# Six places for a delta rule's decay tiles, attention's transposes through a diagonal, and the w_o casts moved into a merge

## The chip, the cores and the metric

The kernel runs on one core of one Trainium2 chip. The metric is device time in microseconds (us) of one execution, as the median of several runs. The core's engines work from their own in-order queues: PE (TensorE, matrix products), DVE (VectorE), ACT (ScalarE), POOL (GpSimd), and SP (SyncE), which here issues nearly all DMAs. An instruction that waits for a semaphore holds everything behind it on its own queue.

## The reference

One layer of a hybrid diffusion backbone: a half-step SwiGLU FFN, two parallel mixers whose results are merged by sigmoid gates, and a second FFN. There are 512 latent tokens, 256 context tokens and 1024 channels. What the change touches is the delta rule, the attention and the merge:

```python
# gated delta rule, by chunks, in two directions, 4 heads
lower = np.tril(np.ones((GDN_CHUNK, GDN_CHUNK), dtype=bool))
decay = jnp.exp(jnp.where(lower, g[..., :, None] - g[..., None, :], -jnp.inf))
m = jnp.where(strict, jnp.einsum('...ik,...jk->...ij', k_beta, k) * decay, 0.0)
uw = lax.linalg.triangular_solve(jnp.eye(GDN_CHUNK) + m, rhs, lower=True, unit_diagonal=True)
...  # scan over the chunks:  o = (q k^T * decay) v_new + (q exp g) S

# neighbourhood attention, 8 heads of 64: 128 local keys in a window and 256 context keys, one softmax
s = jnp.concatenate([s_loc.reshape(bsz, n_heads, width, n_loc), s_ctx], axis=-1).astype(jnp.float32)
p = jax.nn.softmax(s, axis=-1).astype(v.dtype)
return (jnp.einsum('bhwij,bhiwjd->bhwd', p_loc, v_win) + jnp.einsum('bhwn,bhnd->bhwd', p[..., n_loc:], v_ctx))

def branch_merge(o_a, o_b, gate_a, gate_b, w_pa, w_pb, w_o):
    y = jax.nn.sigmoid(gate_a) * (o_a @ w_pa) + jax.nn.sigmoid(gate_b) * (o_b @ w_pb)
    return y @ w_o
```

## The kernel before, in words

The stages follow each other: FFN 1, the input projections, the delta rule's preparation, the delta rule itself (about 743 to 990 us), attention (about 994 to 1093 us), the merge with `w_pa` (1093 to 1120 us), `w_o`, a layer norm, and FFN 2 (to 1529 us). A planner with a cost for each instruction and due times sets the order on every engine once, when the kernel is built; on the chip each engine then keeps that order. Changing one part of the code can therefore move rows of other parts.

Big products are done in three passes: `split` makes of each weight tile `wr` a rounded high part `wh` (a cast on ACT, L135) and a rest `wl` (a subtraction on DVE, L137), and PE multiplies high by high, low by high and high by low (L190, L191, L192). A weight tile takes the way DMA, ACT cast, DVE subtraction, PE.

**Delta rule.** There are three groups (`grams(0)`, `grams(1)`, `grams(2)`) of four grams each, two chunks by two pairs of heads. A gram (`gram`) loads its decays `Dt` from DRAM (`gcd`, L918; 256 KB, each row spread over 128 partitions), subtracts and masks on DVE (four `scalar_tensor_tensor`, L921), exponentiates on ACT (L922), and multiplies PE's products `pq` by it on DVE (`Bt`, L927; for chunks with an output also `At`, L931). `Bt` goes to DRAM (`bd`, L928). After the four grams of a group `base_inverse` reads the blocks back (`Ltr`, `L`, L947), and inverts 32x32 blocks on DVE row by row, in 62 instructions (`bt`, L954, and `Xt`, L955). `Xt` goes through DRAM (`rd`, L959) and comes back as `T` (L976), which DVE transposes (L978), and then PE builds the whole inverse (`pi`, L857). These parts of different groups are interleaved. The tile `Dt` has two buffers for all twelve grams, so gram n+2 loads when gram n has used its own. While this runs, PE does the rest of the input projections as filling work (`fills`, tiles `pm`, written out as `spill` by ACT, L609), until these run out.

**Attention.** 4 pairs of heads `m` by 4 blocks of columns `b` make 16 units. In each, PE makes the scores `sc` (L1240), DVE adds the bias (L1242) and takes the row maximum (L1244), ACT exponentiates into `pr` with the row sums (L1248, twice 128x512), DVE takes the reciprocal `sm` (L1249), POOL multiplies `pr` by it (L1251, twice 128x512), PE transposes `pr` (L1255, eight of 128x128 with `ident`), ACT copies them to `pT` (L1257), and PE multiplies by the values into `po` (L1266). In eight slots between the units PE does a 128x512 product with `w_pb`, and DVE adds it to `yb` (L1302).

**Merge.** Eight products with `w_pa` (a weight of 128x512 each: `wh`, `wl`), a gate on DVE (L1333), an addition to `yb` on POOL (L1334), and the split of `yb` into `yh`, `yl`. The eight weight tiles of `w_o` (128x1024) are also loaded and split here and before (`wso.fill`).

Of the kernel before, what the change touches and what calls it, by code (L numbers as in the profile page):

```python
# [58 lines left out]
def body(ctx, tc, I, out, dbg=None):  # L59
# [72 lines left out]
    def split(src, hi, lo, behind=()):  # L132

        with tc.issue_after(behind[0]) if behind else nullcontext():
            S.copy(hi, src)  # L135
        with tc.issue_after(behind[1]) if behind else nullcontext():
            V.tensor_tensor(lo, src, hi.bitcast(F32), ALU.subtract)  # L137
# [16 lines left out]
    class Stream:  # L154
# [7 lines left out]
        def fill(self, n):  # L162
            while len(self.q) < n and self.i < len(self.srcs):
# [11 lines left out]
                split(raw[:, 0:c], hi[:, 0:c], lo[:, 0:c], self.behind.get(self.i, ()))  # L175
# [737 lines left out]

    def gram(p, s, bd, g):

        mats = mats_of(s)
        Dt = tl(gb_, [P, 4, P], "Dt", 2)
        nc.sync.dma_start(Dt[:], bass.AP(gcd.tensor, gcd.offset + (4 * s + 2 * p) * P, [[0, P], [24 * P, 2], [1, 2 * P]]))  # L918
        for m, (d, c, i) in enumerate(mats):
            msk = cst[:, (C_MF if d == 0 else C_MB):][:, 0:P]  # L920
            V.scalar_tensor_tensor(Dt[:, m], Dt[:, m], gcum[:, d, s, 2 * p + i:2 * p + i + 1], msk, op0=ALU.subtract, op1=ALU.add)  # L921
        S.activation(Dt[:], Dt[:], AF.Exp)  # L922
        Bt, At = tl(gq, [P, 4, P], "Bt", NBT), None
        for n, t in enumerate(products(p, s)):
            if n == 0:
                for m, (d, c, i) in enumerate(mats):
                    V.scalar_tensor_tensor(Bt[:, m], t[m] if s == 1 else t[:, m], beta[:, d, s, 2 * p + i:2 * p + i + 1], Dt[:, m], op0=ALU.mult, op1=ALU.mult)  # L927
# [115 lines left out]
    oaccs = [tl(gq, [P, 4, 2, P], f"oacc{p}") for p in range(2)]  # L1043

    def scan_step(p, s, Tt, At, Sst):
        cf, cb = FWD_CH[s], BWD_CH[s]
        mats = mats_of(s)
        oacc = oaccs[p]
# [32 lines left out]
        if s >= 2:  # L1081
# [10 lines left out]
            if s < 4:  # L1092
                V.tensor_tensor(oacc[:, cf - 2], ot[:, 0:2], o2[:, 0:2], ALU.add)
                V.tensor_tensor(oacc[:, cb - 2], ot[:, 2:4], o2[:, 2:4], ALU.add)
            else:
                V.tensor_tensor(ot[:], ot[:], o2[:], ALU.add)
                G.tensor_tensor(oacc[:, cf - 2], oacc[:, cf - 2], ot[:, 0:2], ALU.add)
                G.tensor_tensor(oacc[:, cb - 2], oacc[:, cb - 2], ot[:, 2:4], ALU.add)
        return Sn

    def gdn_out(p):

        oacc = oaccs[p]
        for t2 in range(2):
            o = oacc[:, 2 * t2:2 * t2 + 2].rearrange("p t i c -> p (t i) c")
# [6 lines left out]
        for i in range(2):  # L1112
            ps = tl(pgq, [P, 4, P], "pc", 2)
            for t in range(4):
                mt(ps[:, t, :], oacc[:, t, i, :], ident)
# [32 lines left out]
    step(base)  # L1148
    scan_of(0, 0)
# [78 lines left out]
    def attend(m, qa, ka, kc, bias, w, between):  # L1228
# [3 lines left out]
        for b in range(4):  # L1232
# [16 lines left out]
            V.reciprocal(sm[:], sm[:])  # L1249
            for i in range(2):  # L1250
                G.tensor_scalar(pr[:, i], pr[:, i], sm[:, i:i + 1], None, op0=ALU.mult)  # L1251
            for i in range(2):
                pt = tl(pg, [P, 4, P], "pt", 2)
                for q in range(4):
                    T.transpose(pt[:, q, :], pr[:, i, q * P:(q + 1) * P], ident)  # L1255
# [74 lines left out]
    for m in range(8):  # L1330
        wso.fill(min(4 + (m + 1) // 2, 7))
        gt, ps = gated("pa", gad, m, oah, oal)
# [358 lines left out]
```

## Time and profile before

| | |
|---|---|
| median of 3 runs | 1527.29 us (1526.62 to 1529.53) |
| the profiled execution | 1530.66 us, its span 1528.8 us, TensorE clock 0.988 |
| busy: PE, weight loads, DVE, ACT, POOL | 1462.6, 1258.7, 1050.0, 605.4, 226.8 us |
| PE / DVE / ACT / POOL busy from 994 to 1094 us (attention) | 92.41, 63.87, 62.49, 63.75 of 100 us |
| PE / DVE / ACT / POOL busy from 1094 to 1120 us (merge) | 23.23, 21.39, 11.67, 10.27 of 26 us |
| POOL's `pr` by `sm`, L1251 | 32 of 1680 ns in the mean, 53.4 us |

A row of the timeline gives the start, the duration, engine, line, operation, output and inputs, the number of instructions joined, and in brackets the idle time of the engine before it and what ended it. A row of the waits gives the engine with its line, what it waited for, the sum in us, the number of waits, and the longest. DMA times run from issue to landing. The share of PE's busy time is a mean over stages with different limits.

### The profile page before, as it was taken

How to read it: one execution, taken by the hardware profiler on the slowest of the kernel's cores; microseconds unless marked ns; L12 is line 12 of the kernel's file. 1: busy time of each engine (PE TensorE's matmuls, PEld its weight loads, DVE VectorE, ACT ScalarE, POOL GpSimd, SP SyncE). 2: the span in 40 equal slices, each digit the busy share in tenths (PEclk: the TensorE clock that was granted, in tenths of full speed). 3: DMA queues.
4: the chain of work that ended last, by engine and by line, in shares of the span. 5: the costliest groups of instructions: out<-in, count | busy, mean ns of one | idle time of the engine just before them, and what ended most of it. 6: DMA issues, size and time to landing. Idle time of an engine off the chain costs nothing.

```text
span 1528.8 us, 23646 instructions
## 1 busy us (share of the span) xinstructions
PE 1462.6 (96%) x9221; PEld 1258.7 (82%) x9221; DVE 1050.0 (69%) x1792; ACT 605.4 (40%) x1005; POOL 226.8 (15%) x224
## 2 busy tenths in 40 slices
PE   6999999999999999999996899999999999999997
PEld 4779988888888887889875778867678999998886
DVE  8765942597554587768777895576669699886426
ACT  5444221322222255546543444266416444344310
POOL 0000000000000011323301001366421022220001
PEclk9999999999999999999998999999999999999999
DMA  9665742667454334222476634283353143333422
GB/s 370 207 237 180 222 142 97 211 213 260 168 192 146 130 112 137 87 90 79 141 216 180 172 99 122 69 284 117 91 174 138 56 139 102 106 110 139 138 83 83
DMA packets 107586, 230.72 MB, mean 151 GB/s; under 512 B 34177, under 2 KB 47825, under 8 KB 107473
## 3 DMA queue, kind: packets, MB, share of 16 engines
q1 hardware_dynamic: 105312, 221.79, 44.7%
q10 hardware_dynamic: 1586, 5.32, 0.9%
q0 software_dynamic: 576, 2.10, 0.4%
q8 instruction: 72, 1.18, 0.3%
q14 instruction: 40, 0.33, 0.1%
HBM read 206.33 MB, written 22.85 MB: 150 GB/s over the span
## 4 chain that ended last, share of the span: by engine, by line
PE 76%; DVE 10%; DMA 7%; issue 3%; ACT 2%; POOL 2%; SPq 0%; DVEq 0%; ACTq 0%; POOLq 0%
PE ps L209 19%; PE ps L190 8%; PE ps L192 8%; PE ps L191 8%; PE pm L190 5%; PE pm L192 5%; PE pm L191 5%; PE pc L857 2%; PE ps L1478 2%; PE ps L1480 2%; PE ps L1479 2%; DVE wl L137 2%; PE po L1266 1%; DMA T<-rd 1%; PE pt L1255 1%
## 5 line engine op out<-in xcount | busy, mean ns | idle before, releaser
L137 DVE TENSOR_TENSOR wl<-wr,wh 128x1024 fp32r<-128x1024 f32 (+1 forms) x215 | 263.0, 1228 | 195.1 <-ACT wh L135 194.3
L135 ACT CAST wh<-wr 128x1024 fp32r<-128x1024 f32 (+1 forms) x215 | 217.8, 1018 | 333.4 <-PE ps L209 105.0
L192 PE MATMUL ps<-uxh,wl 128*128 128x512 f32 (+1 forms) x496 | 179.6, 363 | 2.2 <-DVE wl L137 2.2
L191 PE MATMUL ps<-uxl,wh 128*128 128x512 f32 (+1 forms) x496 | 179.3, 363 | 0.8 <-DVE uxl L137 0.8
L190 PE MATMUL ps<-uxh,wh 128*128 128x512 f32 (+1 forms) x496 | 179.6, 365 | 0.0
L279 DVE SCALAR_TENSOR_TENSOR adap<-wr,crow 128x1024 f32<-128x1024 f32 x112 | 136.8, 1221 | 38.5 <-DMA wr<-in_w_adaT_dram 37.1
L112 POOL TENSOR_TENSOR rs<-ve,mhalf 128x1 f32<-128x1 f32 (+2 forms) x46 | 50.4, 1099 | 744.6 <-DVE ve L108 735.4
L190 PE MATMUL pm<-uxh,wh 128*128 128x512 f32 x320 | 133.0, 416 | 4.1 <-ACT spill L609 2.1
L192 PE MATMUL pm<-uxh,wl 128*128 128x512 f32 x320 | 128.2, 401 | 0.7 <-DVE wl L137 0.7
L191 PE MATMUL pm<-uxl,wh 128*128 128x512 f32 x320 | 127.8, 399 | 0.0
L192 PEld LDWEIGHTS ps<-uxh,wl 128*128 128x128 f32 x496 | 93.7, 189 | 17.9 <-DVE wl L137 3.3
L191 PEld LDWEIGHTS ps<-uxl,wh 128*128 128x128 f32 x496 | 94.0, 189 | 14.9 <-DVE uxl L137 1.0
L190 PEld LDWEIGHTS ps<-uxh,wh 128*128 128x128 f32 x496 | 93.4, 189 | 14.3 <-issue 0.8
L190 PE MATMUL ps<-uch,wh 128*128 128x256 f32 x352 | 98.6, 280 | 0.0
L192 PE MATMUL ps<-uch,wl 128*128 128x256 f32 x352 | 98.3, 279 | 0.0
L191 PE MATMUL ps<-ucl,wh 128*128 128x256 f32 x352 | 98.2, 279 | 0.0
L209 PE MATMUL ps<-wh,hx 128*128 128x512 f32 x352 | 94.8, 389 | 0.0
L209 PEld LDWEIGHTS ps<-wh,hx 128*128 128x128 f32 x352 | 65.9, 188 | 13.6
L190 PEld LDWEIGHTS pm<-uxh,wh 128*128 128x128 f32 x320 | 61.6, 193 | 16.3 <-ACT spill L609 3.0
L192 PEld LDWEIGHTS pm<-uxh,wl 128*128 128x128 f32 x320 | 61.7, 193 | 14.8 <-DVE wl L137 1.5
L191 PEld LDWEIGHTS pm<-uxl,wh 128*128 128x128 f32 x320 | 61.6, 192 | 10.6
L190 PEld LDWEIGHTS ps<-uch,wh 128*128 128x128 f32 x352 | 66.1, 188 | 0.6
(411 smaller groups left out, 3438.7 us busy)
## 6 DMA issues: line engine op xcount, KB each, us to landing
wr<-in_w_adaT_dram SPq DMA_DIRECT2D x88, 512.0 KB, 4.7
wr<-in_up_dram SPq DMA_DIRECT2D x80, 512.0 KB, 4.2
wr<-in_dn_dram SPq DMA_DIRECT2D x58, 512.0 KB, 3.5
wr<-in_win_dram SPq DMA_DIRECT2D x52, 512.0 KB, 3.9
rb<-in_up_dram SPq DMA_DIRECT2D x18, 512.0 KB, 3.7
wr<-in_w_o_dram SPq DMA_DIRECT2D x8, 512.0 KB, 4.0
ac<-in_up_dram SPq DMA_DIRECT2D x6, 512.0 KB, 5.2
Dt<-gcd SPq DMA_DIRECT2D x12, 256.0 KB, 5.1
```

The source lines that it names most:

```text
L112: G.tensor_tensor(rs[:], ve[:], mhalf[:, 0:n], ALU.pow)
L135: S.copy(hi, src)
L137: V.tensor_tensor(lo, src, hi.bitcast(F32), ALU.subtract)
L190: T.matmul(ps, a, uh[:, k, :], start=(k == 0), stop=False)
L191: T.matmul(ps, a, ul[:, k, :], start=False, stop=False)
L192: T.matmul(ps, b, uh[:, k, :], start=False, stop=(k == nk - 1))
L209: T.matmul(banks[t][d][:, c0:c1], a[:, sl], b[:, d * 512 + c0:d * 512 + c1], start=first and j == 0, stop=last and j == 2)
L279: V.scalar_tensor_tensor(pr[:], raw[:], 1.0, crow, op0=ALU.mult, op1=ALU.mult, accum_out=col[:, c:c + 1])
L857: last[0] = T.matmul(*a, **k).ins
L1478: T.matmul(ps[:], a, uh[:, k], start=k == 0, stop=False)
L1479: T.matmul(ps[:], a, ul[:, k], start=False, stop=False)
L1480: T.matmul(ps[:], b, uh[:, k], start=False, stop=k == 3)
```

## The change

It has three parts. First, the decays of the first two grams stay in the two buffers of `Dt`; the next six (grams 2 to 7 in their order) use four tiles `oacc0` to `oacc3` of the same shape, which take the memory of the two output accumulators (before `[P, 4, 2, P]` twice, now `[P, 4, P]` four times), `oacc0` and `oacc1` twice; the last four grams use `Dt` again. The accumulators are taken only after the second group's grams. For the last group the DVE subtraction is ordered behind the `Bt` product of the gram before it. Second, POOL's multiplication of `pr` goes; DVE makes `dg`, `ident` times 1/sum (two `tensor_scalar` of 128x128 per unit), and the eight transposes become matmuls of `pr` with `dg`. Third, in the merge `wso.fill` stands behind `gated`, and each split of a `w_o` tile is ordered behind the split of the latest `w_pa` tile.

```diff
     def gram(p, s, bd, g):
-        Dt = tl(gb_, [P, 4, P], "Dt", 2)
+        k = (None, None, 0, 1, 2, 3, 0, 1, None, None, None, None)[gram_n[0]]
+        gram_n[0] += 1
+        Dt = tl(gb_, [P, 4, P], "Dt", 2) if k is None else tl(gq, [P, 4, P], f"oacc{k}")
...
-            V.scalar_tensor_tensor(Dt[:, m], ...)
+            with tc.issue_after(bt_last[0]) if s > 3 else nullcontext():
+                V.scalar_tensor_tensor(Dt[:, m], ...)
...
-                    V.scalar_tensor_tensor(Bt[:, m], ...)
+                    bt_last[0] = V.scalar_tensor_tensor(Bt[:, m], ...).ins
...
-    oaccs = [tl(gq, [P, 4, 2, P], f"oacc{p}") for p in range(2)]
+    oaccs = [[], []]
+    def out_of(p, c):
+        return oaccs[p][c // 2][:, 2 * (c % 2):2 * (c % 2) + 2]
...
     base = grams(1)
...
+    for k in range(4):
+        oaccs[k // 2].append(tl(gq, [P, 4, P], f"oacc{k}"))
     scan_of(0, 0)
...
             V.reciprocal(sm[:], sm[:])
+            dg = tl(na_, [P, 2, P], "dg", 2)
             for i in range(2):
-                G.tensor_scalar(pr[:, i], pr[:, i], sm[:, i:i + 1], None, op0=ALU.mult)
+                V.tensor_scalar(dg[:, i], ident, sm[:, i:i + 1], None, op0=ALU.mult)
...
-                    T.transpose(pt[:, q, :], pr[:, i, q * P:(q + 1) * P], ident)
+                    T.matmul(pt[:, q, :], pr[:, i, q * P:(q + 1) * P], dg[:, i], start=True, stop=True)
...
     for m in range(8):
+        gt, ps = gated("pa", gad, m, oah, oal)
+        wso.behind = {j: ws.last for j in range(KT)}
         wso.fill(min(4 + (m + 1) // 2, 7))
-        gt, ps = gated("pa", gad, m, oah, oal)
```

Line numbers differ between the two: L918, L921, L927, L928 and L947 before are L924, L928, L934, L935 and L954 after; L954 and L955 are L961 and L962; L959 is L966; L1249 is L1260; L1268 is L1281; L1302 is L1315; L1333 is L1348.

SP's queue where the first group's grams start; `Dt`, `oacc` are loads of decays, `wr` of weights, `qad`, `kad` and `vcd` are stores, `bd0` the stores of `Bt` (the numbers behind a name are those of buffers and versions). Before:

```order
L811 DMA vcd_886_4988<-vcs_1205_6699 128x256
L613 DMA qad_889_4991<-spill_1215_6763 128x512
L613 DMA kad_890_4992<-spill_1220_6797 128x512
L172 DMA wr_1283_7066<-in_win_dram 128x1024
L928 DMA bd0_1221_6800<-Bt_1224_6809 128x4x128
L918 DMA Dt_1233_6867<-gcd_892_4994 128x2x256
L928 DMA bd0_1221_6800<-Bt_1231_6846 128x4x128
L918 DMA Dt_1240_6904<-gcd_892_4994 128x2x256
```

After:

```order
L812 DMA vcd_886_4988<-vcs_1205_6699 128x256
L924 DMA oacc0_1231_6865<-gcd_892_4994 128x2x256
L924 DMA oacc1_1238_6902<-gcd_892_4994 128x2x256
L614 DMA qad_889_4991<-spill_1213_6761 128x512
L924 DMA oacc2_1277_7043<-gcd_892_4994 128x2x256
L924 DMA oacc3_1293_7133<-gcd_892_4994 128x2x256
L614 DMA kad_890_4992<-spill_1218_6795 128x512
L173 DMA wr_1281_7064<-in_win_dram 128x1024
```

Before, the third and fourth load of decays each stand behind the store of a `Bt`; after, they and the next two stand ahead of every store of a `Bt`.

DVE's queue at the same place. Before:

```order
L137 TENSOR_TENSOR wl_1228_6823<-wr_1226_6820,wh_1227_6822 128x1024
L927 SCALAR_TENSOR_TENSOR Bt_1224_6809<-pq_1225_6810,beta_897_5004,Dt_1223_6802 128x128 x4
L927 SCALAR_TENSOR_TENSOR Bt_1231_6846<-pq_1225_6810,beta_897_5004,Dt_1230_6839 128x128 x4
L921 SCALAR_TENSOR_TENSOR Dt_1233_6867<-Dt_1233_6867,gcum_898_5005,cst_896_5002 128x128 x4
L137 TENSOR_TENSOR wl_1238_6888<-wr_1236_6885,wh_1237_6887 128x1024
L921 SCALAR_TENSOR_TENSOR Dt_1240_6904<-Dt_1240_6904,gcum_898_5005,cst_896_5002 128x128 x4
L927 SCALAR_TENSOR_TENSOR Bt_1234_6874<-pq_1235_6875,beta_897_5004,Dt_1233_6867 128x128 x4
L927 SCALAR_TENSOR_TENSOR Bt_1241_6911<-pq_1235_6875,beta_897_5004,Dt_1240_6904 128x128 x4
L137 TENSOR_TENSOR wl_1285_7069<-wr_1283_7066,wh_1284_7068 128x1024
L921 SCALAR_TENSOR_TENSOR Dt_1279_7045<-Dt_1279_7045,gcum_898_5005,cst_896_5002 128x128 x4
L921 SCALAR_TENSOR_TENSOR Dt_1295_7135<-Dt_1295_7135,gcum_898_5005,cst_896_5002 128x128 x4
L927 SCALAR_TENSOR_TENSOR Bt_1280_7052<-pq_1281_7053,beta_897_5004,Dt_1279_7045 128x128 x4
```

After:

```order
L928 SCALAR_TENSOR_TENSOR oacc0_1231_6865<-oacc0_1231_6865,gcum_898_5005,cst_896_5002 128x128 x4
L928 SCALAR_TENSOR_TENSOR oacc1_1238_6902<-oacc1_1238_6902,gcum_898_5005,cst_896_5002 128x128 x4
L137 TENSOR_TENSOR wl_1226_6821<-wr_1224_6818,wh_1225_6820 128x1024
L934 SCALAR_TENSOR_TENSOR Bt_1222_6807<-pq_1223_6808,beta_897_5004,Dt_1221_6800 128x128 x4
L934 SCALAR_TENSOR_TENSOR Bt_1229_6844<-pq_1223_6808,beta_897_5004,Dt_1228_6837 128x128 x4
L928 SCALAR_TENSOR_TENSOR oacc2_1277_7043<-oacc2_1277_7043,gcum_898_5005,cst_896_5002 128x128 x4
L928 SCALAR_TENSOR_TENSOR oacc3_1293_7133<-oacc3_1293_7133,gcum_898_5005,cst_896_5002 128x128 x4
L934 SCALAR_TENSOR_TENSOR Bt_1232_6872<-pq_1233_6873,beta_897_5004,oacc0_1231_6865 128x128 x4
L137 TENSOR_TENSOR wl_1236_6886<-wr_1234_6883,wh_1235_6885 128x1024
L934 SCALAR_TENSOR_TENSOR Bt_1239_6909<-pq_1233_6873,beta_897_5004,oacc1_1238_6902 128x128 x4
L928 SCALAR_TENSOR_TENSOR oacc0_1310_7232<-oacc0_1310_7232,gcum_898_5005,cst_896_5002 128x128 x4
L137 TENSOR_TENSOR wl_1283_7067<-wr_1281_7064,wh_1282_7066 128x1024
```

The four `scalar_tensor_tensor` of the third and of the fourth gram (`oacc0_1231`, `oacc1_1238`) moved from behind the first two `Bt` to ahead of the weight split `wl_1226` (before `wl_1228`), and those of the next grams stand ahead of the `Bt` of the third.

DVE's queue at the end of attention, from the last slot to the last unit's `oa`. Before:

```order
L1302 SCALAR_TENSOR_TENSOR yb_1696_9364<-gt_1936_10492,pm_1937_10494 128x512
L137 TENSOR_TENSOR wl_1950_10561<-wr_1948_10558,wh_1949_10560 128x512
L1249 RECIPROCAL sm_1940_10512<-sm_1940_10512 128x2
L1268 COPY oa_1945_10540<-po_1882_10256 128x512
L137 TENSOR_TENSOR oal_1693_9361<-oa_1945_10540,oah_1692_9360 128x512
```

After:

```order
L1315 SCALAR_TENSOR_TENSOR yb_1698_9366<-gt_1953_10509,pm_1954_10511 128x512
L137 TENSOR_TENSOR wl_1968_10579<-wr_1966_10576,wh_1967_10578 128x512
L1260 RECIPROCAL sm_1957_10529<-sm_1957_10529 128x2
L1264 TENSOR_SCALAR dg_1958_10533<-ident_2_64,sm_1957_10529 128x128 x2
L1281 COPY oa_1963_10558<-po_1896_10270 128x512
L137 TENSOR_TENSOR oal_1695_9363<-oa_1963_10558,oah_1694_9362 128x512
```

The pair of `dg` stands behind the reciprocal; on POOL the multiplications of `pr` are gone.

DVE's queue at the start of the merge: 128x1024 `wl` are of `w_o`, 128x512 `wl` of `w_pa`, `gt` and `yl` of the merge. Before:

```order
L137 TENSOR_TENSOR wl_1955_10586<-wr_1953_10583,wh_1954_10585 128x1024
L137 TENSOR_TENSOR wl_1968_10642<-wr_1966_10639,wh_1967_10641 128x1024
L1333 SCALAR_TENSOR_TENSOR gt_1951_10564<-gt_1951_10564,pm_1952_10566 128x512
L1333 SCALAR_TENSOR_TENSOR gt_1959_10595<-gt_1959_10595,pm_1960_10597 128x512
L137 TENSOR_TENSOR wl_1958_10592<-wr_1956_10589,wh_1957_10591 128x512
L137 TENSOR_TENSOR wl_1963_10617<-wr_1961_10614,wh_1962_10616 128x512
L137 TENSOR_TENSOR wl_1981_10698<-wr_1979_10695,wh_1980_10697 128x1024
L137 TENSOR_TENSOR yl_1947_10554<-yb_1696_9364,yh_1946_10553 128x512 x2
L1333 SCALAR_TENSOR_TENSOR gt_1964_10620<-gt_1964_10620,pm_1965_10622 128x512
L137 TENSOR_TENSOR wl_1971_10648<-wr_1969_10645,wh_1970_10647 128x512
```

After:

```order
L1348 SCALAR_TENSOR_TENSOR gt_1969_10582<-gt_1969_10582,pm_1970_10584 128x512
L1348 SCALAR_TENSOR_TENSOR gt_1974_10607<-gt_1974_10607,pm_1975_10609 128x512
L137 TENSOR_TENSOR wl_1973_10604<-wr_1971_10601,wh_1972_10603 128x512
L137 TENSOR_TENSOR wl_1978_10625<-wr_1976_10622,wh_1977_10624 128x1024
L137 TENSOR_TENSOR wl_1981_10635<-wr_1979_10632,wh_1980_10634 128x512
L137 TENSOR_TENSOR yl_1965_10572<-yb_1698_9366,yh_1964_10571 128x512 x2
L1348 SCALAR_TENSOR_TENSOR gt_1982_10638<-gt_1982_10638,pm_1983_10640 128x512
L137 TENSOR_TENSOR wl_1986_10660<-wr_1984_10657,wh_1985_10659 128x512
L137 TENSOR_TENSOR wl_1991_10681<-wr_1989_10678,wh_1990_10680 128x1024
L1348 SCALAR_TENSOR_TENSOR gt_1987_10663<-gt_1987_10663,pm_1988_10665 128x512
L137 TENSOR_TENSOR yl_1965_10572<-yb_1698_9366,yh_1964_10571 128x512
```

The two splits of `w_o` that opened the merge are gone from its start, and one stands now behind each second `wl` of `w_pa`.

26 lines of the change are left out of this document (13 added, 13 removed).

## The prediction

> **What bounds the kernel now.** I read the page's engine line and chain first, then PE's waits from 700 to 1200 us, then the timeline of the engines at the longest of these waits.
>
> ```profile
> PE 1462.6 (96%) x9221; PEld 1258.7 (82%) x9221; DVE 1050.0 (69%) x1792; ACT 605.4 (40%) x1005; POOL 226.8 (15%) x224
> PE 76%; DVE 10%; DMA 7%; issue 3%; ACT 2%; POOL 2%; SPq 0%; DVEq 0%; ACTq 0%; POOLq 0%
> ```
>
> PE is busy for 1462.6 of 1528.8 us, and 76% of the chain is PE. No PE work of weight is taken away, so the change can only win part of the 66 us in which PE does nothing, and time in which its clock is low.
>
> ```profile
> PE pi L857 <- DMA T<-rd: 13.0, 2, 12.4
> PE po L1266 <- ACT pT L1257: 4.0, 5, 1.9
> PE pm L192 <- DVE wl L137: 3.4, 4, 1.8
> PE pt L1255 <- POOL pr L1251: 1.3, 2, 0.7
> ```
>
> One wait is 12.4 us, for the first group's inverse to come back from DRAM. The next are in attention (`pT`, `pr`) and in the splits of weights. PE around the long wait:
>
> ```profile
> 786.72 0.50 PE L190 MATMUL pm<-uxh,wh 128*128 128x512 f32 x1 [1.53 <-ACT spill L609]
> 787.78 0.50 PE L192 MATMUL pm<-uxh,wl 128*128 128x512 f32 x1 [0.33 <-DVE wl L137]
> 788.55 0.43 PE pm L191
> 791.11 0.43 PE pm L191
> 795.12 0.23 PE pm L191
> 831.15 0.68 PE L857 MATMUL pi<-T,Bt 32*32 32x32 f32 x32 [12.44 <-DMA T<-rd]
> ```
>
> PE loses 1.53 and 0.33 us and then steps at 0.43 instead of 0.23 us for 9 matmuls (787.78 to 791.54: 3.76 us, where 9 x 0.23 is 2.07), together about 3.5 us. Then its filling work ends near 818.7, and it stands still until 831.15. What it waits for is a chain on DVE and SP:
>
> ```profile
> 749.30 0.33 SPq L613 DMA_DIRECT2D qad<-spill  x1
> 777.18 0.37 SPq L918 DMA_DIRECT2D Dt<-gcd  x1
> 818.49 1.47 SPq L947 DMA_DIRECT2D L<-bd  x2
> 820.06 4.31 SPq L959 DMA_DIRECT2D rd<-Xt  x4
> 826.42 2.02 SPq L976 DMA_DIRECT2D T<-rd  x4
> DMA to landing us min/median/max: 4.0/5.1/5.6
> 753.11 2.16 DVE L927 SCALAR_TENSOR_TENSOR Bt<-pq,beta,Dt 128x128 f32<-128x128 f32 x8
> 763.47 2.15 DVE L927 SCALAR_TENSOR_TENSOR Bt<-pq,beta,Dt 128x128 f32<-128x128 f32 x8
> 776.25 0.16 DVE L954 TENSOR_TENSOR bt<-L,Xt 128x2 f32<-128x2 f32 x1 [3.36 <-POOL L L950]
> 783.28 0.88 DVE L921 SCALAR_TENSOR_TENSOR Dt<-Dt,gcum,cst 128x128 f32<-128x128 f32 x3 [3.00 <-DMA Dt<-gcd]
> 794.74 1.14 DVE L921 SCALAR_TENSOR_TENSOR Dt<-Dt,gcum,cst 128x128 f32<-128x128 f32 x4 [1.11 <-DMA Dt<-gcd]
> 807.59 1.14 DVE L921 SCALAR_TENSOR_TENSOR Dt<-Dt,gcum,cst 128x128 f32<-128x128 f32 x4 [0.77 <-DMA Dt<-gcd]
> 817.40 0.69 DVE L955 TENSOR_REDUCE Xt<-bt 128x16 f32<-128x512 f32 x1
> ```
>
> The base inverse runs on DVE from 776.25 to 818.09. Three times in it DVE stands still for a later gram's decays (3.00, 1.11 and 0.77 us), because their load was issued only when a `Dt` buffer came free, and everything behind on DVE's queue waits along: the inverse itself, and the weight splits of the filling work. Then SP sends `rd` at 820.06, after two loads of `L`, and `T` is back 11 us later.
>
> **The change, part 1: places for the decays.** Three terms.
>
> (a) Inside the first inverse DVE's three waits fall away, 4.88 us. In SP's new order the first two of these loads stand right ahead of the store of `qad` (749.30 now) and the next two right behind it; a load lands 5.1 us after its issue. Two of the three groups of four subtractions move ahead of the inverse, 2 x 1.14 us. By DVE alone `Xt` would end at 818.09 - 4.88 - 2.28 = 810.9.
>
> (b) Before the inverse nothing is won. The third and fourth decay are ready earlier, but the `Bt` of these grams waits for PE's products and for four more groups of subtractions put ahead of it. Counted in the new order from 753 with the rows' durations (8 subtractions 2.28, split 1.22, 8 `Bt` 2.15, 8 subtractions 2.28, 4 `Bt`, split, 4 `Bt`), the fourth `Bt` ends between 765.0 and 766, against 763.47 + 2.15 = 765.6. The inverse begins at 776.25 +- 0.5. Here lies a new wait too: the weight split behind `oacc1`'s subtractions. If these loads land at the median (issue near 749.3, plus 5.1) the split is done near 757.9, about when PE asks for it; at 5.6 or later PE stalls by up to 1.2 us.
>
> (c) What sends `rd` is SP's queue, where the loads of the second group's `L` still stand ahead. They need the last `Bt` of that group, hence PE's pace. PE wins the 3.5 us of 786 to 792, and the loads of `Dt` that SP did in the inverse (0.37 us for the one at 777.18) are gone. So `rd` goes at 820.06 - 4.0 = 816.0, and `Xt`, done by 811 to 814, isn't last any more. I take 4.5 us between this and the 4.88 of the waits. PE still waits some 11 to 12 us at the same place, since its filling work ends earlier by as much. Ends: 0, if the inverse comes no earlier, and 7.2, the waits and the moved subtractions together.
>
> After 831 the first two loads of the third group are early as well, but one more group of subtractions falls into a stage where DVE is the busier engine: +0.5. Part 1: -4.0, from +1 to -7.
>
> **Part 2: attention.**
>
> ```profile
> 994.00:1094.00 100.00, 92.41 (x731) 69.84 (x731) 63.87 (x92) 62.49 (x141) 63.75 (x41) 0.97 0.50 171
> 1086.81 0.17 DVE L1249 RECIPROCAL sm<-sm 128x2 f32<-128x2 f32 x1 [2.26 <-ACT pr L1248]
> 1087.14 3.10 POOL L1251 TENSOR_SCALAR pr<-pr,sm 128x512 f32<-128x512 f32 x2 [2.26 <-DVE sm L1249]
> L1255 PEld LDWEIGHTS pt<-ident,pr x128: 137/140/231, 1002.8 to 1091.3; 128*128 128x128 f32 x128
> L857 PEld LDWEIGHTS pq<-kT x48: 187/192/192, 750.6 to 806.5; 128*128 128x128 f32 x48
> 1092.43 0.54 PE L1266 MATMUL po<-pT,vw 128*64 128x128 f32 x5 [0.73 <-ACT pT L1257]
> 1093.45 0.50 PE L190 MATMUL pm<-oah,wh 128*128 128x512 f32 x1
> 751.03 0.89 PE pq L857 x8
> 548.80 0.87 PE ps L146 x8
> L921 DVE SCALAR_TENSOR_TENSOR Dt<-Dt,gcum,cst x48: 340/346/1397, 743.0 to 860.6; 128x128 f32<-128x128 f32 x48
> ```
>
> In the hundred us PE is busy for 92.41, DVE for 63.87, POOL for 63.75. A unit's POOL step takes 3.10 us between reciprocal and transposes. In the middle of the stage the next unit's scores and the `w_pb` products hide it, but for the 1.3 us of `pr` waits. At the end nothing hides it: the last reciprocal ends at 1086.98, and the last `po` at 1093.45.
>
> `dg` on DVE isn't in the trace. A 128x128 operation with two tensor inputs takes 0.346 us here, a reciprocal of 128x2 0.17; with one tensor input I take 0.2 (nearer to the small one, for its size is fixed cost and a little data), so 0.4 per unit, from 0.34 to 0.7. After the last reciprocal then come 0.4 (`dg`), PE's remaining work of the last two units (four transposes, 16 `po`, eight transposes, 16 `po`: 0.11 us for a transpose by the row of eight, 0.073 for a `po` by the 14 between 1092.43 and 1093.45, so 3.6 from 1086.8 on, partly beside `dg`): the end is near 1090.2, 3.3 earlier. The unit before gets its `pT` earlier too, and with it ACT the last exponentials: 0 to 1 more, I take 0.2. The 1.3 us of waits go. The longest wait for `pT`, 1.9 us in the middle of the stage, I leave as it is, since ACT also works on the next pair's loads there; as a bound, a PE without any of its 7.6 idle us in the stage, with its clock at 1.00 instead of 0.97 for half of it, makes -9. DVE's 32 `dg` (6.4 us, 5 to 11) fall on an engine with 36 idle us, behind a reciprocal that waited for the same sums, so nothing on its queue waits for anything new; cover gone, each unit would pay 0.4.
>
> PE: the page's chain has eight transposes (`ps`, L146) at 0.87 us and eight fp32 matmuls of the same shape (`pq`) at 0.89. So 128 x 0.0025 = +0.3. Part 2: -3.3 - 0.2 - 1.3 + 0.3 = -4.5, from -9 to +1 (no wait won, a dearer `dg` shown at the end of the stage).
>
> One rule speaks against this edit. The Trainium skill (TensorE: Matmul & The Clock Gate, Terms) says that the transpose mode of trn2 is four times faster for FP32; by it a matmul in place of a transpose would cost four times the array time. The two rows above, 0.87 and 0.89, don't show it.
>
> **Part 3: the merge.**
>
> ```profile
> 1101.42 0.50 PE L192 MATMUL pm<-oah,wl 128*128 128x512 f32 x1 [0.95 <-DVE wl L137]
> 1114.18 0.50 PE L192 MATMUL pm<-oah,wl 128*128 128x512 f32 x1 [1.78 <-DVE wl L137]
> 1095.88 2.36 DVE L137 TENSOR_TENSOR wl<-wr,wh 128x1024 fp32r<-128x1024 f32 x2 [0.26 <-ACT wh L135]
> 1099.97 4.23 DVE L137 TENSOR_TENSOR wl<-wr,wh 128x512 fp32r<-128x512 f32 x3
> 1112.38 1.75 DVE L137 TENSOR_TENSOR wl<-wr,wh 128x512 fp32r<-128x512 f32 x1
> ```
>
> PE waits here for DVE's `wl`. Two `w_o` splits (2.36 us of DVE, as much of ACT) lay at 1094.8 to 1098.2, ahead of `w_pa` splits that waited for nothing else; this lets the second weight's split come 2 us earlier and may win the 0.95. But three `w_o` splits now stand between `w_pa` splits, each 1.2 us of DVE (half of the 2.36), and more where POOL adds (a split of 128x512 takes 1.75 at 1112.38); PE has 12 x 0.23 = 2.8 us of work per `w_pa` weight. At two of them I expect 1 us of wait each: -0.95 + 2 = +1.0, from -2 (both waits go) to +3.5 (all three shown in full). FFN 2 has the same instructions in slightly another order: 0 +- 1.
>
> **Sum:** -4.0 - 4.5 + 1.0 = -7.5: the profiled execution's 1530.66 gives 1523.2. That one lies 3.4 above the median of the runs; the median becomes 1527.29 - 7.5 = 1519.8.
>
> **The rivals.** 0.2%, 3 us, is about what a measurement of this kernel can tell from no change.
>
> A. *The wait is only moved in part 1.* `L` of the second group, or a weight split held by the decays, sets `rd` as late as now. For it: 820.06 is 2 us behind `Xt`'s end already. Against it: SP's queue itself followed PE's stall at 786. Part 1 gives +0.5; sum -3.0, 1524.3.
>
> B. *Attention's wait passes to ACT.* ACT is busy for 62.49 of the 100 us, and the largest wait is for `pT`, by name ACT's. Against it: in the tail ACT idles until PE has transposed, and that waits for POOL. Then part 2 gives 0 and the sum is -3.0 again, 1524.3.
>
> C. *`w_o` comes late.* All three moved splits show in full beside POOL at twice their 1.2 us (3 x 2.4), less the 0.95: +6 instead of +1, sum -2.5, 1524.8. Against it: after the merge only the eighth tile is cast late, as before.
>
> D. *Slower: the matmul with `dg` streams at a quarter of the transpose's pace.* 0.11 us becomes 0.44, 128 x 0.33 = 42 us on PE, which is the bound in this stage: 1520 + 42 = 1562. It decides from 0.08 us more per matmul, (7.5 + 3) / 128. For it speaks only that the two rows are of different lines; against it, that `po`, fp32 as well, takes 0.073. This is where the skill's rule named above would lead.
>
> E. *The weight load shows.* A weight load of `pq` takes 192 ns, one of `pt` 140. If 0.05 us each were seen, 6.4 us would go: -1.1, 1526.2.
>
> **How the numbers follow.** The forecast has 0.58, with its own range from 1514 to 1523. A 0.12, B 0.09, A and B together 0.06 (1527.8), C 0.06, D 0.04, E 0.05. Faster by over 0.2% means below 1524.2: 0.57 of the forecast, and half of A and B, and cases better than the forecast are in it already, 0.57 + 0.11 = 0.68; a part of C and E with a better attention adds 0.07: 0.75. Slower: D, and 0.05 of what no row names, mostly a merge at its upper end with A and B: 0.09. The rest, 0.16, is the same. The predicted time is the forecast's, 1519.8. The range goes from 1511 (part 1 at -6 and attention at -9, merge -1) to 1526.2, which takes in A, B, C and E (E at its edge).
>
> **What would show it.** PE's wait for `T` at 826 to 827, still 11 to 12 us long, and no wait of DVE for decays between 776 and 815; `rd` sent near 816. If the wait ends at 831, A holds. POOL almost idle in attention, `dg` at 0.2 us, `pt` eight in 0.9 us (D: 3.5 us), the last `po` 4.5 us nearer to the stage's start. In the merge waits for `wl` at the third and fifth `w_pa` weight. I am wrong at the root if PE's time without work after 994 us doesn't shrink although POOL's step is gone.

## The result and the profile after

The changed kernel takes 1538.87 us (median of 6 runs, 1534.77 to 1540.39), the kernel before 1527.22 in the same comparison: a ratio of 1.0072, 95% interval [1.0058, 1.0087]. It is 11.65 us slower, where 7.5 us less had been forecast; the time lies outside the range. The profiled execution took 1538.53 us, with a span of 1536.7.

The page's engine lines after:

```profile
PE 1476.1 (96%) x9349; PEld 1275.9 (83%) x9349; DVE 1056.1 (69%) x1824; ACT 606.5 (39%) x1005; POOL 177.0 (12%) x192
PE 80%; DVE 10%; DMA 5%; issue 2%; SPq 1%; ACT 1%; POOL 1%; DVEq 0%; POOLq 0%; ACTq 0%
```

POOL gave up 49.8 us, as it should. But PE has 128 instructions more than before (9349 against 9221) and is busy 13.5 us longer, though the code replaced 128 PE instructions by 128 others. PE's waits from 700 to 1200 us:

```profile
PE pi L858 <- DMA T<-rd: 12.8, 3, 10.0
PE pi L858 <- DVE Y L1032: 4.9, 3, 2.4
PE pm L193 <- DVE wl L137: 4.2, 5, 1.8
PE pc L858 <- DVE r L1066: 2.8, 3, 1.4
PE pt L1235 <- ACT pT L1270: 1.6, 1, 1.6
PE po L1279 <- ACT pT L1270: 0.4, 1, 0.4
```

The wait for `pr` is gone and that of `po` for `pT` nearly so (4.0 before); 1.6 us of waiting for `pT` stand at the transposes of the values instead. The longest wait for `T` is 10.0 instead of 12.4, but three of them together are as long as two were.

The same stretches of the program in both kernels, by the view of busy time in windows; a row gives start and end, length, then busy time of PE, weight loads, DVE, ACT and POOL with the number of instructions, TensorE's clock, DMA share and GB/s. Before:

```profile
736.30:831.20 94.90, 79.67 (x400) 66.12 (x399) 65.70 (x180) 36.98 (x56) 9.10 (x25) 0.94 0.69 198
831.20:873.50 42.30, 37.92 (x399) 29.83 (x400) 37.29 (x97) 18.27 (x40) 3.91 (x8) 0.94 0.54 159
873.50:921.90 48.40, 46.64 (x496) 38.72 (x495) 42.54 (x125) 20.27 (x45) 3.32 (x9) 1.00 0.35 99
921.90:994.00 72.10, 69.14 (x646) 59.27 (x644) 40.58 (x91) 26.96 (x59) 19.84 (x27) 0.98 0.33 101
994.00:1093.60 99.60, 92.01 (x730) 69.51 (x730) 63.47 (x92) 62.49 (x141) 63.75 (x41) 0.97 0.50 171
1093.60:1131.90 38.30, 35.53 (x151) 27.78 (x152) 27.94 (x29) 13.87 (x20) 14.32 (x10) 1.00 0.53 165
```

After:

```profile
734.20:824.80 90.60, 77.75 (x398) 65.02 (x396) 64.81 (x176) 36.78 (x54) 9.10 (x25) 0.96 0.71 207
824.80:871.80 47.00, 42.09 (x413) 33.32 (x414) 39.33 (x101) 19.53 (x42) 3.61 (x8) 0.93 0.52 151
871.80:924.30 52.50, 48.83 (x494) 40.35 (x493) 42.88 (x128) 19.84 (x46) 3.43 (x9) 0.93 0.31 85
924.30:997.10 72.80, 67.63 (x632) 57.62 (x631) 39.78 (x88) 26.51 (x59) 19.86 (x27) 0.98 0.33 100
997.10:1106.30 109.20, 105.44 (x858) 85.88 (x857) 70.36 (x123) 62.56 (x141) 10.13 (x9) 0.98 0.47 156
1106.30:1144.70 38.40, 34.41 (x144) 26.58 (x145) 27.85 (x29) 13.95 (x20) 15.35 (x10) 1.00 0.52 168
```

The rows run from the first load of decays to the first inverse on PE, from there to the second `rd`, to the third `rd`, to the first scores (these four are the delta rule), to the last `oa` (attention), and to the first gate after `w_o` (merge and the start of `w_o`). The first stage is 4.3 us shorter, near the 4.5 forecast for it. The next two are 4.7 and 4.1 longer, so that attention starts 5.2 later, counted from the first load. Attention is 9.6 longer, with 128 more PE instructions in it. The merge has not moved. What remains to the end is 4.9 shorter in this pair of profiles; over all profiles below it lies between 392.0 and 396.9 us, for the kernel before too at the upper end, and no cause in the change was found for it. Each of these rows is one execution, and the same kernel's stages differ between executions: the changed kernel's second profile, below, has its scores 4.2 us earlier.

The cause in attention stands in one row of the view by tile. `pt` before and after (minimum, median and maximum in ns):

```profile
L1255 PE MATMUL pt<-ident,pr x128: 270/273/477, 1002.8 to 1091.4; 128*128 128x128 f32 x128
```

```profile
L1268 PE MATMUL pt<-dg,pr x256: 270/275/582, 1005.5 to 1104.2; 128*128 128x128 f32 x128
1095.12 2.05 PE L1268 MATMUL pt<-dg,pr 128*128 128x128 f32 x16
L1264 DVE TENSOR_SCALAR dg<-ident,sm x32: 276/281/1121, 1005.2 to 1099.7; 128x128 f32<-128x128 f32 x32
```

There are 128 such matmuls in the code, and 256 records. The "x16" of the timeline are the eight matmuls of one unit, in 2.05 us, where eight transpositions took 0.87 (the row of `ps` in the prediction): a record is about as long as a transposition was, but each matmul has two.

### The profile page after: what moved, and what is told of

Same layout as the page of the kernel before. It is cut to its first block, busy times and chain, and to the rows that moved or that the text cites. A ratio compares the mean times of both kernels' runs of the same rounds, so it can differ in the third digit from the quotient of the medians.

```text
span 1536.7 us, 23860 instructions
## 1 busy us (share of the span) xinstructions
PE 1476.1 (96%) x9349; PEld 1275.9 (83%) x9349; DVE 1056.1 (69%) x1824; ACT 606.5 (39%) x1005; POOL 177.0 (12%) x192
## 4 chain that ended last, share of the span: by engine, by line
PE 80%; DVE 10%; DMA 5%; issue 2%; SPq 1%; ACT 1%; POOL 1%; DVEq 0%; POOLq 0%; ACTq 0%
PE ps L210 22%; PE ps L191 8%; PE ps L193 8%; PE ps L192 8%; PE pm L191 4%; PE pm L193 4%; PE pm L192 4%; PE ps L1493 3%; PE ps L1494 3%; PE ps L1495 3%; PE pc L858 3%; DVE wl L137 2%; PE pt L1268 2%; PE po L1279 1%; DVE bt L961 1%
## 5 line engine op out<-in xcount | busy, mean ns | idle before, releaser
L280 DVE SCALAR_TENSOR_TENSOR adap<-wr,crow 128x1024 f32<-128x1024 f32 x112 | 136.8, 1221 | 38.4 <-DMA wr<-in_w_adaT_dram 37.0
L210 PE MATMUL ps<-wh,hx 128*128 128x512 f32 x352 | 94.8, 389 | 0.0
```

The source lines that it names most:

```text
L210: T.matmul(banks[t][d][:, c0:c1], a[:, sl], b[:, d * 512 + c0:d * 512 + c1], start=first and j == 0, stop=last and j == 2)
L280: V.scalar_tensor_tensor(pr[:], raw[:], 1.0, crow, op0=ALU.mult, op1=ALU.mult, accum_out=col[:, c:c + 1])
```

## The experiments

All times are medians; the kernel before lay between 1527.1 and 1527.4 us in every comparison. Each kernel also left a profile, so that the same stages could be compared over many kernels. Edits are against the kernel before, if nothing else is said.

### Each part alone, and the matmul by itself

The four kernels are: the decays' part alone (the places together with the rule that orders the last group's subtractions), attention's part alone, the merge's part alone (each is its hunk of the diff), and, for the matmul by itself,

```diff
-                    T.transpose(pt[:, q, :], pr[:, i, q * P:(q + 1) * P], ident)
+                    T.matmul(pt[:, q, :], pr[:, i, q * P:(q + 1) * P], ident, start=True, stop=True)
```

> Only the places for the decays. Theory M (in the changed kernel the matmul with a diagonal costs two passes on PE, and that is the loss): this part alone does not lose, it gives 0 to -5 us; T is back near 821 as in the changed kernel's profile and the scores of attention start no later than before (994). Rival G (the decays' part loses: its lead of 6.4 us at 831 turns into a delay of 3.1 at the start of attention in the changed kernel's profile): +3 us, scores at 997.

Measured: 1533.65, ratio 1.0041 [1.0026, 1.0057]: +6.3 us, more than even rival G said. But the place differs: the first inverse is at 90.8 us after the first decay load (94.9 before), and the scores are at 256.2 (257.7), so in this profile the delta rule lost nothing. Attention, whose code is unchanged, took 103.9 us (99.6), with PE busy 3.8 us longer at a granted clock of 0.92 (0.97). The merge took 43.0 (38.3). About half of that is in ACT's order, in the timeline of this kernel:

```profile
1095.28 2.00 ACT L135 CAST wh<-wr 128x1024 fp32r<-128x1024 f32 x2
1101.03 2.09 ACT L135 CAST wh<-wr 128x1024 fp32r<-128x1024 f32 x3 [3.76 <-DMA wr<-in_w_o_dram]
1102.64 0.50 PE L190 MATMUL pm<-oah,wh 128*128 128x512 f32 x1 [3.00 <-ACT wh L135]
1094.00:1137.00 43.00, 37.95 (x151) 29.85 (x152) 27.98 (x30) 13.77 (x20) 14.31 (x10) 0.92 0.46 145
```

The planner, with other times ahead of it, put a `w_o` cast whose load had not landed before two `w_pa` casts. This is what the third part of the change forbids. In the last row, the same stretch as the last one before, PE is idle for 5.1 us instead of 2.8; but it is also busy for 37.95 instead of 35.53 us, with the same 151 instructions, at a clock of 0.92 instead of 1.00. So the order cost some 2.3 us here and the clock as much.

> Only attention's part: POOL's scaling gone, dg on DVE, transposes as matmuls with dg. Theory M: 128 matmuls x 2 records x 0.11 us = 14 us more PE, less the idle time that POOL's step left (4 to 5 us): +8 to +11 us. Rival G: within 3 us of before.

Measured: 1534.12, 1.0042 [1.0026, 1.0057]: +6.7 us, a little under theory M's band and far from G's.

> Only the merge's part: the w_o splits behind those of w_pa. Theories M and G alike: 0, within 2 us; a value beyond +3 would mean that the moved splits hold PE (rival C of the prediction).

Measured: 1525.68, 0.9992 [0.9978, 1.0006]: no difference that can be told, at most a gain of 3.4 us. The merge took 38.4 us.

> Before, with one edit: the eight transposes of a unit are plain fp32 matmuls with the same ident; POOL's scaling stays. This is the disputed cost by itself. Theory M: 256 PE records instead of 128, eight matmuls in 1.75 instead of 0.87 us, and +9 to +14 us in all (14 if PE is the bound all through attention). Rival (a plain matmul costs what a transpose costs, as the prediction had it): within 1 us of before.

Measured: 1540.44, 1.0086 [1.0071, 1.0102]: +13.1 us, with 256 records; attention took 112.2 us with PE busy in 107.8 of them. The same data, the same `ident`, the same shape: the price is that of the plain matmul. Attention's whole part at +6.7 then holds a gain of 6.3 for POOL's step, if the two add; in the two profiles attention itself is 3.0 us shorter for it (109.1 against 112.2).

### What the matmul costs, and the step that POOL held

The decays' and the merge's part with attention undone; DVE in POOL's place (`V.tensor_scalar(pr...)` for `G.tensor_scalar(pr...)`, transposes as before); the same edit with the decays' and the merge's part; and the changed kernel with

```diff
-            pr = tl(na_, [P, 2, 512], "pr", 2)
+            pr = tl(na_, [P, 2, 512], "pr", 2, F32R)
-            dg = tl(na_, [P, 2, P], "dg", 2)
+            dg = tl(na_, [P, 2, P], "dg", 2, F32R)
```

> The changed kernel with pr and dg as fp32r, so that the matmul with dg is one fp32r pass; pr is rounded to fp32r in it, which the changed kernel doesn't do. If the two records per fp32 matmul are the price, then 128 records instead of 256 and eight in 0.9 us: -11 to -14 us against the changed kernel, 1525 to 1528. Rival (the price is that of a plain matmul of this shape, whatever its type): 1537 to 1540.

Measured: 1528.56, 1.0009 [0.9997, 1.0020] against the kernel before, 10.3 us less than the changed kernel. The row of `pt`:

```profile
L1268 PE MATMUL pt<-dg,pr x128: 272/276/476, 1003.9 to 1093.1; 128*128 128x128 f32 x128
```

128 records. So it is fp32 that makes two, not the plain matmul, and with the second record go 10.3 of the 11.65 us. This kernel also ran at a lower granted clock, 0.984 in the median of its runs where the changed kernel and the one before have 0.988 to 0.989, so at an equal clock the difference would probably be larger.

> Before, with one edit: DVE scales pr (twice 128x512 per unit) in POOL's place; transposes as before. If the step that POOL held was worth 6.3 us (the matmul with ident alone cost 13.0 us, attention's whole part 6.7), this gives -4 to -6 us. Rival: DVE becomes the wait of the stage (32 more operations), within 2 us of before.

Measured: 1523.44, 0.9982 [0.9970, 0.9993]: -3.7 us. The scaling takes 480 ns per 128x512 in the median on DVE; POOL needed 1563.

```profile
L1251 DVE TENSOR_SCALAR pr<-pr,sm x32: 474/480/1341, 1003.6 to 1087.2; 128x512 f32<-128x512 f32 x32
```

> The changed kernel with attention's part undone (POOL's scaling and plain transposes back). Theory S (the places for the decays win 1 to 4 us by the end of the delta rule, and the 6.3 us that they lost alone came later, from the planner's new order of the merge's casts, which the third part pins): 1522 to 1527, with a merge of 38 us or less from the last oa to the first h1 (43 in the kernel with the decays' part alone). Rival D (the decays' part itself costs time in the delta rule): 1531 to 1533, scores 259 us or more after the first decay load (256.2 there, 257.7 before).

Measured: 1530.52, 1.0026 [1.0009, 1.0043], between the two: the merge was 38.4 as theory S had it, but the scores came 261.4 us after the first load, as D had it. So the decays' part, its rule included, does cost time by itself: 4.8 us against the merge's part alone.

> The changed kernel with DVE scaling pr and plain transposes, without dg. If the three causes add (decays and merge together 0 to -5 us, POOL's step -4 to -6): 1517 to 1523, faster than both. Rival: the planner's order spends it again, 1526 or more.

Measured: 1527.33, 0.9998 [0.9987, 1.0009]. The rival's figure: DVE's scaling gives 3.2 us, the decays' part spends it.

### What in the decays' part costs time

Four kernels: the merge's part with DVE's scaling and no places; then the decays' and the merge's part without the rule (`with nullcontext():` in place of `issue_after(bt_last[0]) if s > 3`); with places for the third and fourth gram only; and with places for the second group only.

> Before, with two edits: the merge's part of the change, and DVE scaling pr in POOL's place with plain transposes; no places for the decays, no dg. If the causes add (merge -1.4, POOL's step -3.7): 1521 to 1523, faster than before and than the changed kernel. Rival: 1526 or more, because the planner's order changes with it.

Measured: 1520.05, 0.9956 [0.9941, 0.9971]: -7.0 us, the best of all kernels here.

> The decays' and the merge's part without the rule that orders the third group's subtractions behind the Bt of the gram before. In that kernel with the rule three of the last four groups of subtractions lie between the first T and the second rd, where DVE is the bound (45 us against 42.6 without places). Theory V (DVE's work moved into that stage is what spends the lead): here two of the four lie ahead of the first inverse, so that stage takes 43 to 44 us, and the whole 1 to 3 us less than the 1530.5 with the rule. Rival L (what spends it is the third group's loads and L, which stay as late): the stage stays at 45, time 1529 to 1532.

Measured: 1525.85, 0.9987 [0.9973, 1.0000]: 4.7 us less than with the rule. Both theories missed. V said the direction, but the stage from the first `T` to the second `rd` stayed at 45.1 us; L said the stage but not the time. DVE's extra group of subtractions in that stage isn't the cause: two groups lie in it here, as in the kernel before, and it is no shorter than with three.

> The decays' and the merge's part, but only the third and fourth gram have places of their own; the second group uses the two Dt buffers again. If the 4.4 us at the first T come from the loads inside the first inverse, this gives 0 to 1 of them (T 95 us after the first decay load), and the time lies near that of the merge's part alone, 1525 to 1528. Rival (they come from the first group's earlier subtractions): T at 91 to 92.

Measured: 1538.15, 1.0069 [1.0049, 1.0090]. The first `T` came at 95.1 us, as expected: the lead comes from the loads inside the first inverse. The time was missed by 10 us and more; its stages after `T` were 45.6, 52.3 and 67.9 us. It is the slowest of these. Its runs had a granted clock of 0.985 in the median, which is a part of it by the estimate below the table; no run showed why.

> The decays' and the merge's part, but only the second group's four grams have places of their own; the third and fourth gram use Dt. Loads inside the first inverse are early here, so T at 91 to 92 us after the first decay load as with all six places; by theories V and L the time stays near 1529 to 1531, since the stages after T lose it as before. Rival: the loss came from the first group's order, then 1521 to 1524.

Measured: 1531.37, 1.0023 [1.0009, 1.0038], `T` at 91.4 us: as expected, the second group's places alone give the lead, and it is spent.

### The rule by itself

> The merge's part and the rule alone: the third group's subtractions ordered behind the Bt of the gram before, without any places of their own. Theory R (it is this rule that spends the lead; without it the places cost nothing): 1529 to 1531 against 1525.7 of the merge's part alone, the first T at 95 to 96 us as without places, and the stage from the first T to the second rd at 45 us with three groups of subtractions in it. Rival P (the places cost it, the rule only together with them): 1524 to 1527.

Measured: 1530.68, 1.0022 [1.0011, 1.0033]: +5.0 us from the rule alone, with `T` at 94.4 us. Theory R holds in the time; in the place it is off by one stage, for the time from the first `T` to the second `rd` is 43.0, and that to the third `rd` is 53.7 (48.0 with the merge's part alone). DVE's waits in that third stage, of the merge's part alone, and with the rule added:

```profile
DVE bt L955 <- POOL L L951: 2.1, 1, 2.1
```

```profile
DVE wl L137 <- ACT wh L135: 6.6, 2, 5.9
```

With the rule the planner builds another order of what follows; in it DVE stands 5.9 us before a weight split. These are two single executions, of 1523.4 and 1533.2 us, further apart than the medians. In the changed kernel the same time goes to another wait, for the third group's `L`:

```profile
DVE bt L961 <- POOL L L957: 5.6, 1, 5.6
```

> Places without the rule, the merge's part, and DVE scaling pr with plain transposes. By adding (1525.9 without the rule, -3.2 for POOL's step): 1521 to 1523. If the places are worth their 4 us at the first T once nothing later spends them: 1515 to 1518, faster than the 1520.1 without places. Rival: the planner's order spends it, 1525 or more.

Measured: 1522.46, 0.9979 [0.9966, 0.9992]: what adding gives. Against the same kernel with the rule (1527.33) it is 4.9 us less. The places are worth nothing to the whole even without the rule; the same kernel without them took 1520.05.

> The changed kernel with one edit: the rule on the third group's subtractions taken out. Theory R: -4 to -5 us against the changed kernel, 1534 to 1535, since the two records of the matmul stay. Rival P: within 1.5 us of 1538.9.

Measured: 1533.33, 1.0046 [1.0032, 1.0060]: 5.5 us less than the changed kernel. Theory R, in the changed kernel itself.

> The changed kernel once more, for a second profile of its stages: attention 109 us within 1, merge 38.4, the delta rule 259 to 263 us from the first decay load to the scores, and the first T at 90 to 92.

Measured: 1535.34 us (one run), `T` at 90.3 and a merge of 38.4 as expected; the scores at 258.7 and attention at 110.3 lie 0.3 us outside what was expected.

The profiles together, in us; the first four numbers are stages of the delta rule, as in the windows above, and the clock is the granted one in attention. The last column is an estimate over all runs of a kernel: one minus the granted clock of a run, times its span, is the TensorE time that a lower clock withheld, and the mean over the runs is given.

| kernel | to first T | to 2nd rd | to 3rd rd | to scores | delta rule | attention | clock in it | median time | withheld by the clock |
|---|---|---|---|---|---|---|---|---|---|
| before | 94.9 | 42.3 | 48.4 | 72.1 | 257.7 | 99.6 | 0.97 | 1527.2 | 16.4 |
| merge's part | 96.1 | 42.9 | 48.0 | 71.0 | 258.0 | 96.7 | 1.00 | 1525.7 | 16.3 |
| merge's part, DVE scales | 96.0 | 41.5 | 49.0 | 71.2 | 257.8 | 96.4 | 0.98 | 1520.1 | 16.5 |
| DVE scales | 94.8 | 42.3 | 49.9 | 72.3 | 259.3 | 96.1 | 0.98 | 1523.4 | 17.8 |
| attention's part | 95.6 | 43.0 | 47.5 | 69.7 | 255.9 | 109.1 | 0.98 | 1534.1 | 14.0 |
| matmul with `ident` | 96.2 | 42.7 | 47.8 | 70.9 | 257.6 | 112.2 | 0.98 | 1540.4 | 16.9 |
| merge's part and rule | 94.4 | 43.0 | 53.7 | 70.5 | 261.6 | 103.4 | 0.93 | 1530.7 | 17.7 |
| places, no rule, merge's part | 90.5 | 45.1 | 51.3 | 68.9 | 255.8 | 104.1 | 0.92 | 1525.9 | 16.3 |
| the same, DVE scales | 89.8 | 45.2 | 51.1 | 69.5 | 255.6 | 97.0 | 0.96 | 1522.5 | 16.2 |
| changed kernel, no rule | 89.6 | 45.4 | 51.3 | 69.0 | 255.3 | 110.1 | 0.97 | 1533.3 | 14.8 |
| places and rule | 90.8 | 44.9 | 49.4 | 71.1 | 256.2 | 103.9 | 0.92 | 1533.7 | 22.6 |
| places, rule, merge's part | 91.9 | 44.9 | 51.1 | 73.4 | 261.4 | 101.0 | 0.97 | 1530.5 | 20.1 |
| the same, DVE scales | 91.2 | 44.9 | 51.4 | 71.2 | 258.7 | 95.2 | 0.98 | 1527.3 | 19.5 |
| places for the 3rd and 4th gram, rule, merge's part | 95.1 | 45.6 | 52.3 | 67.9 | 260.9 | 101.9 | 0.97 | 1538.2 | 22.8 |
| places for the 2nd group, rule, merge's part | 91.4 | 46.0 | 50.8 | 71.6 | 259.7 | 103.5 | 0.93 | 1531.4 | 19.1 |
| changed kernel with fp32r | 91.3 | 45.3 | 51.4 | 73.2 | 261.2 | 99.6 | 0.91 | 1528.6 | 24.3 |
| changed kernel, two profiles | 90.6, 90.3 | 47.0, 46.1 | 52.6, 51.0 | 72.8, 71.3 | 262.9, 258.7 | 109.2, 110.3 | 0.98, 0.97 | 1538.9 | 17.7 |

Without the rule the places win 4 to 6 us at the first `T`, and up to the scores the three profiles take 255.3 to 255.8 us, where those without places and rule take 255.9 to 259.3: little is kept. With places and rule it is 256.2 to 262.9, so mostly nothing is left.

## Why the prediction was wrong, point by point

**Attention, -4.5: wrong, it was +6.7.** The step that failed is the price of the matmul. The prediction read "eight fp32 matmuls of the same shape (`pq`)" out of the row "0.89 PE pq L857 x8". They were four: `products` makes four for each gram, the 24 of `kT` with `kT` show up as x48 in the view by tile, and that row stood in the prediction itself. The row gives 0.22 us for a matmul, against 0.11 for a transposition, and the term is 128 x 0.11 = 14 us instead of 0.3; alone it measured +13.1. The other terms of that sum were about right in size: POOL's step and its waits -4.8 forecast, -6.3 by the difference of attention's part and the matmul alone, and 3.2 to 5.6 won where DVE took the step with the transposes kept. `dg` takes 0.28 us, not 0.2, and the weight loads of `pt` waited for it 0.3 us in all.

So rival D came true at a third of its price, 0.11 us more per matmul instead of 0.33. That is above its point of decision, 0.08; its chance of 0.04 was too low. The argument against it, that `po` takes 0.073 though it is fp32 as well, had the same slip: the code has 128 such matmuls, and the trace before has 256 records.

```profile
L1266 PE MATMUL po<-pT,vw x128: 272/273/476, 1008.3 to 1092.8; 128*64 128x128 f32 x128
L1266 PE MATMUL po<-pT,vc x128: 272/273/421, 1008.8 to 1093.2; 128*64 128x128 f32 x128
```

The rule of the Trainium skill named in the prediction (TensorE: Matmul & The Clock Gate, Terms) points the right way: a transposition is cheaper than an fp32 matmul, here by two, not four. The prediction set it aside on the strength of a miscounted row.

**The decays, -4.0: wrong, it was +4.8.** Step (a) held: DVE's three waits in the inverse went, and it took 34.6 us (777.02 to 811.64; 36.2 in the second profile) instead of 41.8, up to the whole 7.2 of the waits and the moved subtractions (4.88 and 2.28). Its end, the way of `rd` and PE's first inverse after:

```profile
810.96 0.68 DVE L962 TENSOR_REDUCE Xt<-bt 128x16 f32<-128x512 f32 x1
814.81 4.36 SPq L966 DMA_DIRECT2D rd<-Xt  x4
824.78 0.69 PE L858 MATMUL pi<-T,Bt 32*32 32x32 f32 x32 [9.96 <-DMA T<-rd]
```

Step (b), that nothing changes ahead of the inverse, did not hold. Its start at 777.0 looks close to 776.25, but this execution reached its first load of decays 2.1 us earlier than the one before (734.2, not 736.3). Counted from that load the inverse starts after 42.8 us instead of 40.0; in all profiles with places it is 42.4 to 46.3, without them 39.2 to 40.6. The store of the first group's last `Bt` goes no later (28.9 us after the load, 29.4 before), but its reading back does (`Ltr`, 35.2 against 33.8). That the loads of decays now around that store delay it is likely, and was not tested.

Step (c) came out near its figure, but not by its reason. `rd` still waited for SP's queue behind `L`. It went at 814.81 (816.0 forecast), counted from the first load 3.2 us earlier than before (4.0 forecast), and from there to PE's first inverse it took 10.0 us instead of 11.1, for which no cause in the change was found. PE did not win the 3.5 us of 786 to 792. Its waits for `spill` and `wl` between the first load and the end of its filling work are as long after as before (2.9 and 2.8 us together), and the slow steps were no wait at all: the granted clock was 0.50, as the view in windows of the kernel before shows. The waits before, then after, and that row:

```profile
PE pm L190 <- ACT spill L609: 2.1, 2, 1.5
PE pm L192 <- DVE wl L137: 0.7, 2, 0.3
PE pm L191 <- ACT spill L610: 1.9, 1, 1.9
PE pm L193 <- DVE wl L137: 1.0, 2, 0.6
789.00:790.00 1.00, 1.00 (x3) 0.78 (x3) 0.90 (x4) 0.00 (x0) 0.00 (x0) 0.50 1.14 184
```

So that the stage was 4.3 us shorter (4.5 forecast), and 4 to 6 in most profiles with places, is partly luck: what the inverse won was in part lost ahead of it, and the rest came by other ways than the sum had.

The term that failed is "+0.5" for all that comes after the first `T`. From the first `T` to the scores the two profiles of the changed kernel took 172.3 and 168.4 us, the one before 162.8: +9.5 and +5.6; without the rule it is 165.3 to 165.8, +2.5 to +3. (In the decays' part alone, which has the rule, it is 165.4; there the loss came later.) I priced one group of subtractions and not the rule behind it. The rule orders the last group's subtractions; it looks like a detail, but it cost 5.0 us when added to a kernel without places, and 4.7, 4.9 and 5.5 less was measured when it was taken out of three kernels with them. What I had missed besides: a lead at one wait of PE is worth only what the next waits leave of it. The stages of the next two inverses take another 91 us before, and were 1 to 5 us longer each in every kernel with places, with or without the rule.

**The merge, +1.0: within its band.** -1.7, not told from none; with all parts 38.4 us as before. None of the moved splits held PE noticeably. Its use appeared only beside the decays' part, where by the medians it is worth 3.1 us (1533.65 and 1530.52).

**The sum.** -7.5 was forecast. By the runs it is about +13 (the matmul), -6 (POOL's step), +5 (the rule), -1.7 (the merge) and 0 (the places): about 10, and 11.65 was measured.

What stays open is how the rule costs 5 us on the chip. A part goes with a lower granted clock. By the estimate in the table's last column the clock withheld more with the rule than without it in each of the four pairs: 1.4, 3.8, 3.3 and 2.9 us, each uncertain by about 1 us. (In the decays' part alone it is 6.2 us more than before, about as much as that kernel lost.) Why the clock is lower there, no run shows. The rest doesn't sit at one place: in the kernel with the rule alone DVE waits 5.9 us for a cast at the start of the third inverse; in the changed kernel DVE waits 5.6 us for `L`. That each follows from another order of the whole queue is argued, not shown. The attention of kernels with POOL's step took 96.7 and 99.6 us without places and rule, at clocks of 1.00 and 0.97, and 101.0 to 104.1 with either of them, at 0.92 to 0.97; with DVE scaling it took 95.2 to 97.0 in all.

## What to carry to other kernels

Count a row's instructions against the code before dividing by its "x": 256 records for 128 calls, or 48 for 24, show the double price in plain sight. An fp32 multiplication that is merged into a transposition isn't free when the transposition is one record and the multiplication two; scaling the operand on an engine with room (DVE, 0.48 us per 128x512 here) won 3.2 to 5.6 us with the transposes left as they were. And where a planner sets the order, test a rule on the order alone: one line on the order of sixteen subtractions cost about 5 us in four pairs of kernels, and the places that it served won nothing. Count from an event near the stage, not from the start of the execution, when two profiles are compared, and look at the granted clock before a longer stage is put down to the code.

## What the runs showed of the hardware that I had not expected

A plain fp32 matmul of 128x128 by 128x128 is two records on PE and 0.22 us; with both operands as fp32r it is one record; a transposition of fp32 is one record and 0.11 us. The weight load takes 192 ns in the median for a plain matmul of either type and 140 for a transposition, but back to back this doesn't show in the step: at full clock a transposition follows the one before it by 109 ns in the median, a record of the fp32 matmul by 112, one of the fp32r matmul by 113.

In one execution the granted clock can matter more than idle time: in the kernel with places but without the rule, attention had 730 PE instructions and a clock of 0.92 and took 104.1 us, and in that with the merge's part alone, also with 730, a clock of 1.00 and 96.7 us. PE was idle 8.3 and 7.4 us, but busy 95.83 and 89.31. The medians of the two kernels are 1525.85 and 1525.68, so a difference of 7 us in one stage of one profile need not be one of the kernels.

```profile
989.40:1093.50 104.10, 95.83 (x730) 73.20 (x730) 64.55 (x92) 62.92 (x141) 63.69 (x41) 0.92 0.48 164
```

```profile
991.90:1088.60 96.70, 89.31 (x730) 67.50 (x730) 63.93 (x92) 62.25 (x141) 63.50 (x41) 1.00 0.53 176
```
